# Output projection of a hybrid decoder block: a fifth pair of weight tiles by seven products, its loads and two groups of small attention products moved

## The chip, the cores and the metric

The kernel runs on one core of one Trainium2 chip. The core has a matrix engine (TensorE, PE in the profile; its weight loads are PEld), a vector engine (VectorE, DVE), a scalar engine (ScalarE, ACT), GpSimd (POOL), a synchronizing engine (SyncE, SP) that here issues nearly all loads, and 16 DMA engines. The metric is the device time in microseconds of the whole program, as the median of several runs; lower is better.

## The reference

One decoder block on 256 tokens of width 2048, all in float32. The part that matters here:

```python
proj = x @ w_in                       # split into GLA q/k/v/gate, FoX q/k/v/forget, two merge gates
y_gla = o @ w_branch_gla              # gated linear attention, 4 heads
y_fox = of @ w_branch_fox             # forgetting attention, 8 heads, softmax with a bias from cumsum(log f)
merged = sigmoid(ma) * y_gla + sigmoid(mb) * y_fox
mix = merged @ w_out                  # the output projection, 2048 x 2048
x = layer_norm(ALPHA * x + mix, ln1_g, ln1_b)
ffn = conv_gated_mlp(x, ...)          # w_gate, w_up: 2048 x 5632, w_down: 5632 x 2048
x = layer_norm(ALPHA * x + ffn, ln2_g, ln2_b)
x = x + sigmoid(x @ w_ple_gate) * (p @ w_ple_proj)
```

## The kernel before

**Precision and tiles.** Every large product is made of three products in the type fp32r: each operand is split into a high part (`copy` on ScalarE writes `hi`) and the rest (`tensor_tensor` on VectorE writes `lo`), and hi*hi, hi*lo and lo*hi are summed. The weights stream through SBUF as units of 128 x 2048 values (`wu`, 1 MB). `unit()` (line 235) hands out the next unit and first prepares those up to three ahead (`prep`, line 191): SP loads two raw tiles of 128 x 1024 into a ring of four, ScalarE makes hi, VectorE lo.

**Two kinds of large product.** `w_unit` (lines 290 and 292) has the weights as the stationary operand: for each of 16 blocks one matmul of hi against 512 columns (high and low part of the activations) and one of lo against 256. The input projections (tiles psfq, psfk, psq, psk, psm), the branches (psa, psb) and the feed-forward's gate and up use it. `x_mm` (line 334) has the activations as the stationary operand and weight rows of 512 columns as the moving one; values, output gates, the output projection (wo) and the down projection (dn) use it, through `x_half`, which does 1024 output columns at a time in four PSUM banks, two token blocks by two column blocks. In `x_half` a unit is a pair of 128-row blocks of the weights; a half of the output projection is 8 pairs.

**A pair by seven products.** A pair is a 2 x 2 by 2 x 2 block product, 8 block products of 3 matmuls, 24 in all. For the pairs listed in `WOW` for the output projection and `DNW` for the down projection, `seven` (line 354) computes it by seven block products of 3 matmuls, in Strassen's manner. That needs sums of the activation blocks (`x_sums`, line 363, made in the branch loop when the pair's second block is done, and kept in `msums`, two tiles of two pairs each), combined weights, and four more PSUM tiles `ms`, which gather over the half's listed pairs and are added into the residual z by `joined` (lines 1095 to 1117) after the last of them. The output projection's combined weights are made during the loop over the merge gates: `combs_gen` (line 896) takes three calls per listed pair: load 1 MB (combw, SP), two subtractions, a third one and a store to DRAM (tfd, POOL's queue). It is called once per gate column block from number 17 on, 32 in all, then in the branch loop. `prep_seven` (line 142) then loads, for such a pair, 256 KB (rawl), 512 KB (raw) and the 1 MB of combined weights (full), in that order, and splits them into hi, lo and two tiles ts.

**Buffers.** One tag, S8, has 15 buffers of 128 x 2048 values. During the output projection it holds the merged activations mT (4), one tile of sums ms1, the tiles full and ts of listed pairs (1 and 2 each), the two token blocks z1 of the residual, the normalization's gain and bias rows (lnb, 2), later its output x1T (4). Another, t2, has six buffers of 128 x 512.

**The order of the work.** The instructions of all engines but SP are put in order by a scheduler at build time, by priority (the order of the program) and by when it expects operands and buffers. SP's instructions stay in program order. What is to happen between pairs is given to `x_half` as a table `mid`: the entry of pair i runs after pair i's products were issued. In line 1268 these are, for the output projection's first half, the loads of the residual's two token blocks (`mid1`, SP) after pairs 2 and 3 and of the gain row (`mid1g`, POOL's queue) after pair 6; for the second half the bias row after pair 1 and other loads after pair 3.

**The small products.** While the large projections run, `pull(1)` after each unit advances a list of generators. `gates_gen` (line 599) does one GLA head's decay gates per call (psg, line 579, two small fp32r products each) and, in a call after the four heads, `fox_columns` (line 562): two fp32 transposes (pct) of the cumulative forget gate and a copy on ScalarE. `fox_gen` (line 609) sweeps the eight heads of the forgetting attention: in the call of head h it transposes its weights (`turn`, pt), forms the logits of head h + 1 (pl) and the value products of head h - 1 (`values`, po); two calls per head, so that the last head's value products have a call of their own, two units after its transposes.

Of the kernel before, what the change touches and what calls it, by code (L numbers as in the profile page):

```python
# [10 lines left out]
F32R = mybir.dt.float32r  # L11
# [8 lines left out]
P = 128  # L20
# [4 lines left out]
H = 4  # L25
DK = 256
FH = 8
# [18 lines left out]
DNP = (1, 2, 4, 5, 7, 8, 10, 11, 13, 14, 16, 18)  # L46
DNW = (DNP, DNP[1:-1])
WO0 = 120
WOW = ((1, 2, 4, 5), ())
WOP = tuple(sorted(set(WOW[0] + WOW[1])))  # L50
COMBW = 17
COMB0 = 13
# [12 lines left out]
def tile_block(ctx: ExitStack, tc: tile.TileContext, wu, xw, wfv, wpp, xT_in, x_in, pT_in, wlr,  # L65
# [7 lines left out]
    sm = ctx.enter_context(tc.tile_pool(name="sm", bufs=2))  # L73
# [9 lines left out]
    st1 = [cst.tile([P, 4, 6], F32, name=f"st1{t}") for t in range(2)]  # L83
# [53 lines left out]
    tsd = dr.tile([len(units7), P, 1024], F32, name="tsd")  # L137
    units7w = [WO0 + nh * 8 + i for nh in range(2) for i in WOW[nh]]
    tsw = {u: j for j, u in enumerate(units7w)}
# [422 lines left out]
    def fox_columns():  # L562
        pct = mxtile("pct")
        for t in range(2):
            nc.tensor.transpose(pct[:, 8 * t:8 * t + FH], zc_[:, t * P:t * P + P],
                                ident[:FH, :FH])
        copy(ct, pct[:, 0:2 * FH])
# [7 lines left out]
    def gla_gates(h):  # L575
        psg = mxtile(f"psg{h}")
        for c in range(2):
            n = (2 * h + c) * P
            nc.tensor.matmul(psg[:, c * 256:c * 256 + 256], lhsT=wS[:, n:n + P],
                             rhs=gS, start=True, stop=True)  # L580
        z = t2("z")
        for c in range(2):
            nc.scalar.activation(z.rearrange("p (t c n) -> p t c n", t=2, c=2)[:, :, c, :],
                                 psg[:, c * 256:c * 256 + 256].rearrange("p (t n) -> p t n", t=2),
                                 AF.Identity, scale=1.0,
                                 bias=chn[:, c_blr + 2 * h + c:c_blr + 2 * h + c + 1])
        g = t2("g")
        log_sigmoid(z, g, P, 512)
        nc.vector.tensor_tensor_scan(gb[:, h, 0:256], reset, g[:, 0:256], 0.0,
                                     ALU.mult, ALU.add)  # L590
        b1 = gb[:, h, 256:512].rearrange("p (c n) -> p c n", n=P)
        nc.vector.tensor_tensor_scan(gb[:, h, 257:512], reset[:, 0:255], g[:, 256:511], 0.0,
                                     ALU.mult, ALU.add)
        nc.vector.memset(b1[:, :, 0:1], 0.0)
        nc.vector.tensor_tensor(gt[:, h, :, :], b1[:, :, 127:128],
                                g[:, 256:512].rearrange("p (c n) -> p c n", n=P)[:, :, 127:128],
                                ALU.add)

    def gates_gen():
        for h in range(H):  # L600
            gla_gates(h)
            yield
        fox_columns()

    mixers.append(gates_gen())

# [2 lines left out]
    def fox_gen():  # L609


        lgs, sts, ptss = {}, {}, {}
        halves = ((256, 128), (0, 256))

        def logits(h):
            pl = mxtile(f"pl{h}")
            for t, (o, n) in enumerate(halves):
                nc.tensor.matmul(pl[:, o:o + n], lhsT=fq[:, h, t * P:t * P + P],
                                 rhs=fk[:, h, 0:n], start=True, stop=True)
            lg = lgs[h] = t2("lg")[:, 0:384]  # L620
            for t, (o, n) in enumerate(halves):
                nc.vector.scalar_tensor_tensor(lg[:, o:o + n], pl[:, o:o + n],
                                               ct[:, t * FH + h:t * FH + h + 1],
                                               ncb[:, h * 256:h * 256 + n], ALU.add, ALU.add)
            nc.vector.tensor_tensor(lg[:, P:384], lg[:, P:384], cmask, ALU.add)
            st = sts[h] = sm.tile([P, 8], F32, tag="fst", name="fst")
            nc.vector.tensor_reduce(st[:, 0:1], lg[:, 256:384], AX.X, ALU.max, negate=True)
            nc.vector.tensor_reduce(st[:, 1:2], lg[:, 0:256], AX.X, ALU.max, negate=True)

        def softmax(h):  # L630
            lg, st = lgs[h], sts.pop(h)
            for t, (o, n) in enumerate(halves):
                nc.scalar.activation(lg[:, o:o + n], lg[:, o:o + n], AF.Exp,
                                     bias=st[:, t:t + 1], scale=1.0,
                                     accum_out=st[:, 2 + t:3 + t])
            nc.vector.reciprocal(st[:, 4:6], st[:, 2:4])
            for t, (o, n) in enumerate(halves):
                nc.vector.tensor_scalar(lg[:, o:o + n], lg[:, o:o + n], st[:, 4 + t:5 + t],
                                        None, ALU.mult)

        def turn(h):
            lg = lgs.pop(h)
            pt = mxtile(f"pt{h}")
            for i, d in enumerate((1, 2, 0)):
                nc.tensor.transpose(pt[:, d * P:d * P + P], lg[:, i * P:i * P + P], ident)
            pts = ptss[h] = t2("pts")[:, 0:384]
            copy(pts, pt[:, 0:384])

        def values(h):
            pts = ptss.pop(h)  # L650
            po = mmtile(f"po{h}")
            nc.tensor.matmul(po[:, 0:256], lhsT=fv[:, 0, h * P:h * P + P], rhs=pts[:, 0:256],
                             start=True, stop=False)
            nc.tensor.matmul(po[:, 128:256], lhsT=fv[:, 1, h * P:h * P + P],
                             rhs=pts[:, 256:384], start=False, stop=True)
            dst = ofT[h // 4][:, h % 4, :]
            copy(dst[:, 0:256], po[:, 0:256])
            nc.vector.tensor_tensor(dst[:, 256:512], po[:, 0:256],
                                    dst[:, 0:256].bitcast(F32), ALU.subtract)

        logits(0)
        yield
        softmax(0)
        yield
        for h in range(FH + 1):
            if h < FH:
                turn(h)
            if h + 1 < FH:
                logits(h + 1)
            if h > 0:  # L670
                values(h - 1)
            if h + 1 < FH:
                softmax(h + 1)
            yield
            yield

# [18 lines left out]
    for nm, dst, sc in (("q", gq, 1.0 / 16.0), ("k", gk, 1.0)):  # L695
        for n in range(8):
# [3 lines left out]
            h, c = n // 2, n % 2  # L700
# [224 lines left out]

    msums = [lt([P, 2, 2, 512], F32R, "hT10"), s8([P, 2, 2, 512], F32R, name="ms1")]

    def m_sums(i):
        j = WOP.index(i)
        return msums[j // 2][:, j % 2, 0, :], msums[j // 2][:, j % 2, 1, :]  # L930

    for nh in range(2):
# [3 lines left out]
    mT = [s8([P, 4, 512], F32R, name=f"mT{i}") for i in range(4)]  # L936
    fhl = None
    ya_even = None
    for n in range(16):
# [6 lines left out]
        j = n % 2  # L946
# [197 lines left out]
    def ple_prep(half):  # L1144

        if half == 0:
            praw = s8([P, 2, 1024], name="praw")
        w = [s8([P, 2048], F32R, name=f"pw{half}{i}") for i in range(2)]
        pt_ = s8([P, 2, 512], F32R, name=f"pTs{half}")
        pTs = [pt_[:, k, :] for k in range(2)]  # L1150
        for k in range(2):
            if half == 0:
                raw = praw[:, k, :]
            else:
                raw = ring.tile([P, 1024], F32, tag="raw", bufs=4, name=f"praw{half}{k}")
            nc.sync.dma_start(raw, wpp[half, :, k * 1024:k * 1024 + 1024])
            o = slice(k * 1024, k * 1024 + 1024)
            copy(w[0][:, o], raw)
            nc.vector.tensor_tensor(w[1][:, o], raw, w[0][:, o].bitcast(F32), ALU.subtract)
        pT = t2("pTr").rearrange("p (k t) -> p k t", t=S)  # L1160
        nc.sync.dma_start(pT, pT_in)
        for k in range(2):
            copy(pTs[k][:, 0:256], pT[:, k, :])
            nc.vector.tensor_tensor(pTs[k][:, 256:512], pT[:, k, :],
                                    pTs[k][:, 0:256].bitcast(F32), ALU.subtract)
        return w, pTs

    z1 = [s8([P, 2048], name=f"z1{t}") for t in range(2)]
    gain = [None, None]

    def mid1(t):
        nc.sync.dma_start(z1[t], x_in[t])
# [3 lines left out]
    def mid1g(i):  # L1176
        gain1.append(load_row(0, i))

    x1T = []
    pq, first = [], []  # L1180

    def mid1x():
        x1T.extend(s8([P, 4, 512], F32R, name=f"x1T{g}") for g in range(4))
# [81 lines left out]
                    turn1(G[3])  # L1265
            first.extend(ps)

    residual("wo", mT, 16, z1, st1, ({2: lambda: mid1(0), 3: lambda: mid1(1), 6: lambda: mid1g(0)}, {1: lambda: mid1g(1), 3: lambda: (pq.append(ple_prep(0)), mid1x())}), end=end1, ws=WOW)
    mixers.append(affine(z1, gain[0], lambda t: nc.gpsimd.dma_start(x1d[t], z1[t]),
                         [g for g in range(4) if g not in AFF_DVE]))  # L1270

# [99 lines left out]
    pb, pq = [], []  # L1371
# [224 lines left out]
```

## Time and profile before

| | |
|---|---|
| median of three runs | 1652.53 us (1652.47 to 1653.07) |
| the profiled execution's own time | 1651.61 us |
| its span in the profile | 1649.8 us |
| TensorE busy | 1643.6 us |
| TensorE weight loads / VectorE / ScalarE busy | 1426.9 / 1233.6 / 882.2 us |
| granted TensorE clock | full speed (1.0) |

A profile is one execution. The page gives each engine's busy time, the chain of work that ended last and the costliest groups of instructions. Other views of the same trace, which the prediction uses: the waits of an engine (who waited for whom), the instructions in order of time (start, duration, engine, line, operation, output <- input, count; in brackets the idle time before and what ended it), the busy time in given stretches, and the DMA issues with size and time to landing. A matmul's duration reaches into the next one, since matmuls are pipelined; the distance between two starts is what one costs.

### The profile page before, as it was taken

To read this page: it belongs to the slowest core of one execution; us is meant where nothing else is said; L and a number is where in the kernel's file an instruction comes from. 1 tells how busy PE (TensorE), PEld (TensorE's weight loads), DVE (VectorE), ACT (ScalarE), POOL (GpSimd) and SP (SyncE) were. 2 spreads that over 40 slices of the span, in tenths; PEclk is the share of its full clock that TensorE was granted. 3 is DMA by queue.
4 is the path that set the end of the run, shared out by engine and by line. 5 is a ranking of instruction groups with operands and counts; after the bars stand their busy time and mean duration, and the time that the engine had idled before them with its cause. 6 is when DMAs were issued, how large, how long until landed. Compare 5 with 4: busy or idle time off the path is not lost.

```text
span 1649.8 us, 24319 instructions
## 1 busy us (share of the span) xinstructions
PE 1643.6 (100%) x8956; PEld 1426.9 (86%) x8956; DVE 1233.6 (75%) x1819; ACT 882.2 (53%) x1268; POOL 94.8 (6%) x219
## 2 busy tenths in 40 slices
PE   9999999999999999999999999999999999999998
PEld 8988888888888888888888888888888888888887
DVE  6666658668856667786888778888887688788784
ACT  6745545445555455555565545555455566466643
POOL 0000000000000000000010011111110011010000
PEclk9999999999999999999999999999999999999999
DMA  7765555555555685668747678889886589799354
GB/s 299 233 196 189 168 186 178 183 179 179 174 180 195 242 307 192 193 206 316 267 155 234 232 257 334 316 325 337 322 285 229 192 292 325 270 329 363 141 187 170
DMA packets 107527, 394.23 MB, mean 239 GB/s; under 512 B 12504, under 2 KB 13408, under 8 KB 104464
## 3 DMA queue, kind: packets, MB, share of 16 engines
q1 hardware_dynamic: 97008, 352.62, 62.0%
q0 software_dynamic: 10256, 39.86, 6.3%
q8 instruction: 70, 1.15, 0.3%
q14 instruction: 49, 0.40, 0.1%
q10 hardware_dynamic: 144, 0.20, 0.0%
HBM read 365.36 MB, written 27.27 MB: 238 GB/s over the span
## 4 chain that ended last, share of the span: by engine, by line
PE 96%; DMA 2%; ACT 1%; DVE 1%; issue 0%; SPq 0%; ACTq 0%
PE psu L290 9%; PE psg L290 9%; PE dn L334 7%; PE psm L290 7%; PE gv L334 5%; PE gr L334 5%; PE pg L334 5%; PE psu L292 5%; PE psg L292 5%; PE psm L292 4%; PE psa L290 3%; PE wo L334 3%; PE dn L354 3%; PE fv L496 3%; PE dn0m L354 2%; PE psfq L290 2%
## 5 line engine op out<-in xcount | busy, mean ns | idle before, releaser
L217 DVE TENSOR_TENSOR lo<-raw,hi 128x1024 fp32r<-128x1024 f32 x502 | 611.5, 1224 | 271.9 <-ACT hi L212 270.3
L212 ACT ACTIVATE hi<-raw 128x1024 fp32r<-128x1024 f32 x502 | 528.7, 1059 | 465.4 <-DMA raw<-in_wu_dram 114.6
L290 PE MATMUL psu<-x1T,hi 128*128 128x512 f32 x688 | 236.0, 389 | 0.0
L290 PE MATMUL psg<-x1T,hi 128*128 128x512 f32 x672 | 230.5, 389 | 0.0
L292 PE MATMUL psu<-x1T,lo 128*128 128x256 f32 x688 | 189.9, 276 | 0.0
L292 PE MATMUL psg<-x1T,lo 128*128 128x256 f32 x672 | 185.5, 276 | 0.0
L290 PE MATMUL psm<-xT,hi 128*128 128x512 f32 x512 | 175.5, 390 | 0.0
L290 PEld LDWEIGHTS psu<-x1T,hi 128*128 128x128 f32 x688 | 129.1, 188 | 26.7
L290 PEld LDWEIGHTS psg<-x1T,hi 128*128 128x128 f32 x672 | 126.2, 188 | 26.1
L292 PE MATMUL psm<-xT,lo 128*128 128x256 f32 x512 | 141.4, 276 | 0.0
L292 PEld LDWEIGHTS psu<-x1T,lo 128*128 128x128 f32 x688 | 129.2, 188 | 0.0
L292 PEld LDWEIGHTS psg<-x1T,lo 128*128 128x128 f32 x672 | 126.1, 188 | 0.0
L290 PEld LDWEIGHTS psm<-xT,hi 128*128 128x128 f32 x512 | 96.1, 188 | 19.9
L334 PE MATMUL dn<-hi,hT 128*128 128x512 f32 x352 | 97.8, 389 | 0.0
L292 PEld LDWEIGHTS psm<-xT,lo 128*128 128x128 f32 x512 | 96.2, 188 | 0.2
L290 PE MATMUL psa<-oT,hi 128*128 128x512 f32 x256 | 87.8, 389 | 0.0
L334 PEld LDWEIGHTS dn<-hi,hT 128*128 128x128 f32 x352 | 66.0, 188 | 13.7
L292 PE MATMUL psa<-oT,lo 128*128 128x256 f32 x256 | 70.7, 276 | 0.0
L334 PE MATMUL gr<-hi,xT 128*128 128x512 f32 x256 | 70.6, 392 | 0.0
L334 PE MATMUL gv<-hi,xT 128*128 128x512 f32 x256 | 70.4, 391 | 0.0
L334 PE MATMUL pg<-hi,x2T 128*128 128x512 f32 (+1 forms) x224 | 60.0, 376 | 0.0
L290 PEld LDWEIGHTS psa<-oT,hi 128*128 128x128 f32 x256 | 48.1, 188 | 10.1
(357 smaller groups left out, 3070.4 us busy)
## 6 DMA issues: line engine op xcount, KB each, us to landing
raw<-in_wu_dram SPq DMA_DIRECT2D x528, 512.0 KB, 4.9
comb<-in_wu_dram SPq DMA_DIRECT2D x22, 768.0 KB, 8.9
tsd<-comb POOLq DMA_DIRECT2D x22, 512.0 KB, 7.3
top<-tsd SPq DMA_DIRECT2D x22, 512.0 KB, 5.8
fvraw<-in_wfv_dram SPq DMA_DIRECT2D x15, 524.0 KB, 7.9
rawf<-in_wu_dram SPq DMA_DIRECT2D x14, 512.0 KB, 9.5
top<-in_wu_dram SPq DMA_DIRECT2D x22, 256.0 KB, 6.8
hi<-hsd POOLq DMA_DIRECT2D x22, 256.0 KB, 4.9
```

The lines of the kernel that those rows point to most:

```text
L212: c = nc.scalar.activation(hi, raw, AF.Copy, bias=0.0, scale=1.0)
L217: return nc.vector.tensor_tensor(lo, raw, hi.bitcast(F32), ALU.subtract)
L290: nc.tensor.matmul(ps, lhsT=hi[i // 8 if hoff == 0 else 0][:, w0 % 1024:w0 % 1024 + P], rhs=a[:, kt % 4, :], start=first and i == 0, stop= ...
L292: nc.tensor.matmul(ps[:, 256:512], lhsT=lo[i // 8 if hoff == 0 else 0][:, w0 % 1024:w0 % 1024 + P], rhs=a[:, kt % 4, 0:256], start=False, ...
L334: nc.tensor.matmul(bs[j][:, 0:m], lhsT=x, rhs=v[:, o:o + m], start=first and i == 0, stop=last and i == 2)
L354: nc.tensor.matmul(ps, lhsT=a, rhs=v, start=m and first and i == 0, stop=m and last and i == 2)
L496: nc.tensor.matmul(fbk[t][c][:, 0:n], lhsT=x, rhs=w[:, o:o + n], start=kt == 0 and i == 0, stop=kt == 15 and i == 2)
```

## The change

The list of the output projection's first half gains pair 6. Its activation sums get two tiles of the tag t2 (`ms2`), its weights are combined in a fifth round of `combs_gen`, and its four extra PSUM tiles go on gathering for one more pair, so that `joined` runs after pair 6 and not after pair 5. In the table of the output projection's loads, both token blocks of the residual move to after pair 4, the gain row to after pair 0 of the second half, the bias row to after its pair 2. `fox_columns` runs ahead of the last head's gates, in the same call. The last head's value products are issued in the call of its own transposes, so `fox_gen` ends one head step sooner.

```diff
-WOW = ((1, 2, 4, 5), ())
+WOW = ((1, 2, 4, 5, 6), ())
...
     def gates_gen():
         for h in range(H):
+            if h == H - 1:
+                fox_columns()
             gla_gates(h)
             yield
-        fox_columns()
...
-        for h in range(FH + 1):
-            if h < FH:
-                turn(h)
+        for h in range(FH):
+            turn(h)
             if h + 1 < FH:
                 logits(h + 1)
             if h > 0:
                 values(h - 1)
             if h + 1 < FH:
                 softmax(h + 1)
+            else:
+                values(h)
             yield
             yield
...
+    ms2 = [sm.tile([P, 512], F32R, tag="t2", bufs=6, name=nm) for nm in ("ms2h", "ms2l")]
+
     def m_sums(i):
         j = WOP.index(i)
+        if j == 4:
+            return ms2
         return msums[j // 2][:, j % 2, 0, :], msums[j // 2][:, j % 2, 1, :]
...
-    residual("wo", mT, 16, z1, st1, ({2: lambda: mid1(0), 3: lambda: mid1(1), 6: lambda: mid1g(0)}, {1: lambda: mid1g(1), 3: lambda: (pq.append(ple_prep(0)), mid1x())}), end=end1, ws=WOW)
+    residual("wo", mT, 16, z1, st1, ({4: lambda: (mid1(0), mid1(1))}, {0: lambda: mid1g(0), 2: lambda: mid1g(1), 3: lambda: (pq.append(ple_prep(0)), mid1x())}), end=end1, ws=WOW)
```

## The prediction

> **What bounds the kernel now.** I read the page first, then TensorE's waits, then TensorE's instructions in order of time around the output projection, and last the queues and engines that feed it there.
>
> ```profile
> span 1649.8 us, 24319 instructions
> ...
> PE 1643.6 (100%) x8956; PEld 1426.9 (86%) x8956; DVE 1233.6 (75%) x1819; ACT 882.2 (53%) x1268; POOL 94.8 (6%) x219
> ...
> PE 96%; DMA 2%; ACT 1%; DVE 1%; issue 0%; SPq 0%; ACTq 0%
> ```
>
> ```profile
> PE wo L334 <- DVE lo L217: 0.2, 1, 0.2
> ```
>
> TensorE is busy for all but 6.2 us of the span and holds 96% of the chain that ends last. So two things shorten this kernel: fewer products, or products that follow each other faster. One of TensorE's few waits lies where the change works (wo). A busy TensorE can still hide short delays, so I use the distances between starts.
>
> ```profile
> 754.48 0.39 PE L354 MATMUL wo<-hi,hT 128*128 128x512 f32 x1
> ...
> 759.24 0.39 PE L354 MATMUL wo<-hi,hT 128*128 128x512 f32 x1
> ...
> 764.00 0.62 PE L334 MATMUL wo<-hi,mT 128*128 128x512 f32 x2
> ...
> 769.44 0.39 PE L354 MATMUL wo<-hi,ms 128*128 128x512 f32 x1
> ...
> 778.96 1.07 PE L334 MATMUL wo<-hi,mT 128*128 128x512 f32 x4
> ...
> 782.57 0.73 PE L334 MATMUL wo<-lo,mT 128*128 128x512 f32 x2 [0.21 <-DVE lo L217]
> ...
> 784.52 1.07 PE L334 MATMUL wo<-hi,mT 128*128 128x512 f32 x4
> ```
>
> Pair 1 (seven products) runs from 754.48 to 759.24 and pair 2 to 764.00: 4.76 us each, 21 matmuls of 0.227. Pair 3, plain, runs to 769.44: 5.44 us, 24 matmuls of 0.227. Pair 6, plain, starts at 778.96; its 23rd matmul starts at 784.52, 5.56 later, where 22 x 0.227 = 4.99 are due. So pair 6 loses 0.57 us, more than the 0.2 that the waits show.
>
> **Pair 6 by seven products: TensorE.** It drops from 24 matmuls to 21: 3 x 0.227 = **-0.68 us**, on the path, since nothing but matmuls fills it. The Trainium skill (TensorE: Matmul & The Clock Gate, section Back-to-back issue gap) gives about 131 ns per matmul of 512 columns as a sustained rate in real kernels; by it the term would be an estimated -0.39. The rows above, 4.76 over 21 and 5.44 over 24, do not agree with that figure, and the rows decide.
>
> **Pair 6: the stall of 0.57.** Where does it come from?
>
> ```profile
> 755.97 0.42 SPq L1172 DMA_DIRECT2D z<-in_x_dram  x1
> ...
> 759.97 0.44 SPq L149 DMA_DIRECT2D full<-tfd  x1
> 760.46 0.43 SPq L1172 DMA_DIRECT2D z<-in_x_dram  x1
> 760.99 34.09 SPq L205 DMA_DIRECT2D raw<-in_wu_dram  x12
> ```
>
> ```profile
> 766.38 1.07 POOL L1138 DMA_DIRECT2D lnb<-in_lng_dram  x2 [171.24 <-DVE ts L160]
> ```
>
> ```profile
> 760.00:765.00 5.00, 5.00 (x24) 4.14 (x23) 2.97 (x4) 2.83 (x3) 0.00 (x0) 1.00 1.01 415
> ...
> 775.00:780.00 5.00, 5.00 (x24) 4.02 (x23) 1.23 (x1) 1.06 (x1) 0.00 (x0) 1.00 1.00 413
> ```
>
> ```profile
> 780.20 1.06 ACT L212 ACTIVATE hi<-raw 128x1024 fp32r<-128x1024 f32 x1 [1.70 <-DMA raw<-in_wu_dram]
> ...
> 783.61 0.58 ACT L1109 ACTIVATE ju<-wo0m 128x512 f32<-128x512 f32 x1
> ```
>
> The last two columns of the stretches are the DMA engines' share and their GB/s: they are full, at some 415 GB/s, while pair 6's raw tiles, issued at 760.99, stand behind the two z (the residual's token blocks) and pair 5's full tile, and beside two rows lnb (the normalization's gain and bias); its second half reaches ScalarE only at 780.20. The change moves both z loads (SP) behind pair 6's own loads and ahead of pair 7's, and both lnb loads to the second half. Those are on POOL's queue, whose 171 us of idle time before them show that nothing stands behind them.
>
> ```profile
> raw<-in_wu_dram SPq DMA_DIRECT2D x53, 512.0 KB, 4.9
> full<-tfd SPq DMA_DIRECT2D x4, 1024.0 KB, 7.1
> z<-in_x_dram SPq DMA_DIRECT2D x2, 1024.0 KB, 11.0
> ...
> rawl<-in_wu_dram SPq DMA_DIRECT2D x4, 256.0 KB, 5.6
> ```
>
> Pair 6 now brings raw 0.5 + rawl 0.25 + full 1.0 = 1.75 MB instead of 1.0, but has lost 2 MB of z in front: 1.25 MB less, at 415 GB/s 3.0 us earlier than the 780.2 above.
>
> ```profile
> L217 DVE TENSOR_TENSOR lo<-raw,hi 128x1024 fp32r<-128x1024 f32 x502 | 611.5, 1224 | 271.9 <-ACT hi L212 270.3
> ```
>
> So its last tile lands by 777.2 even if lnb goes out as early as now, and up to 2/0.415 = 4.8 us before that if not. Its four splits of 1024 columns take 1.06 each on ScalarE and 1.22 on VectorE, side by side; the last two (ts), ready by 777.2 + 1.06 + 2 x 1.22 = 780.7, are first read by the tenth matmul, at 778.96 + 9 x 0.227 = 781.0. **The stall goes: -0.57.** Next to be late is pair 7, with 0.75 MB more ahead of it, 1.8 us if lnb goes as early as now. Its raw tiles follow those at 780.2, its need is 778.96 + 4.76 = 783.72: up to 0.5 us could come back. I take 0.
>
> **Joining moves one pair later.** The first of its operations is ScalarE's copy ju (L1109). It ran at 783.61, 4.65 after pair 5's end at 778.96, since it stood behind the late raw tiles in ScalarE's order. Pair 6 now ends at 783.72, so it can start where it started.
>
> ```profile
> 787.82 0.68 DVE L1106 TENSOR_TENSOR ju<-ju,wo0m 128x512 f32<-128x512 f32 x1
> ```
>
> The second PSUM bank that the next half needs comes free with the read at 787.82, at 788.5. The next half began at 790.41 (784.97 + 5.44) and would begin at 789.16: 0.66 us of cover instead of 1.9. I take 0, and 0.5 for the range.
>
> **What pair 6 adds off the path.** Another combine pass (1 MB in, 1 MB out, three VectorE operations) on the last three rounds of the gate loop; its sums on VectorE and ScalarE in the branch loop, whose tiles ms2 take two of six t2 buffers that nothing else needs there.
>
> ```profile
> 600.00:610.00 10.00, 10.00 (x61) 8.86 (x60) 6.42 (x8) 5.41 (x8) 0.00 (x0) 1.00 0.81 296
> 736.00:745.00 9.00, 9.00 (x55) 7.98 (x54) 7.12 (x12) 5.96 (x9) 0.00 (x0) 1.00 0.80 274
> ```
>
> ```profile
> L363 DVE TENSOR_TENSOR msf<-ya x8: 291/292/293, 646.7 to 720.1; 128x128 f32<-128x128 f32 x8
> ...
> L969 DVE SCALAR_TENSOR_TENSOR ms<-msf,ms x2: 684/684/684, 707.8 to 724.1; 128x512 fp32r<-128x512 f32 x2
> ```
>
> The sums are 4 x 0.29 + 0.68 = 1.85 us on VectorE, which stands idle 1.9 of the 9 us from 736 to 745: hidden, barely. The pass has 19% of the DMA engines free from 600 to 610. Both at 0; without cover 0.5 each.
>
> **The order of the small products.** The two fp32 transposes of the forget columns (pct) move one round up, beside the last gates; the last head's value products (po) move up beside its transposes. No product is added or dropped. But the trace shows what a visit of such products can leave behind:
>
> ```profile
> L290 PE MATMUL psfq<-xT,hi 128*128 128x512 f32 x46 | 16.1, 395 | 0.0
> L292 PE MATMUL psfq<-xT,lo 128*128 128x256 f32 x46 | 12.9, 280 | 0.0
> ```
>
> ```profile
> L290 PE MATMUL psk<-xT,hi 128*128 128x512 f32 x31 | 10.9, 395 | 0.0
> L292 PE MATMUL psk<-xT,lo 128*128 128x256 f32 x31 | 8.7, 280 | 0.0
> ```
>
> ```profile
> L290 PE MATMUL psk<-xT,hi 128*128 128x512 f32 x75 | 25.5, 389 | 0.0
> L292 PE MATMUL psk<-xT,lo 128*128 128x256 f32 x74 | 20.4, 276 | 0.0
> ```
>
> These are the same matmuls from 82 to 104 (behind pct), from 204 to 214.6 (behind the visit of turn and values) and from 217 to 242 (behind the last visit). In the first two windows a pair of hi and lo takes 6 + 4 = 10 ns longer, and it stays so until another visit. The 46 + 31 = 77 pairs cost 0.77 us; psfq is followed by psfk in the first window, so I count about 1 us in all. What sets it I can't read from the trace; it follows the visits, and the change alters just these two.
>
> ```profile
> 80.62 0.28 PE L565 MATMUL pct<-ident,zc 8*128 8x8 f32 x2
> 80.84 0.50 PE L290 MATMUL psfq<-xT,hi 128*128 128x512 f32 x1
> ```
>
> The visit itself costs 0.22 us and a first matmul 0.11 longer than 0.39; sharing a visit saves 0.1 to 0.2 at each place, unless the values wait for ScalarE's copy of the transposes and become a visit of their own again. Bounds: best -1.3 (both slow stretches gone, visits shared); worst, the last visit leaves the slow pace on the 75 pairs that now run fast: +0.75, say 0.8. I take **-0.5**, half of the slow pace gone.
>
> **The sum**, against the profiled execution's own 1651.61 (span 1649.8 and 1.81 around it): -0.68 - 0.57 - 0.5 = -1.75, so 1649.9. The runs' median, 1652.53, lies 0.92 above that execution; the same step down gives **1650.8**.
>
> **The rivals.** *The slow pace stays or spreads* (for: nothing in the trace says which order is quick; against: the last visit, values alone, leaves the fast pace): -1.25 with 0 to +0.8, up to 1652.1. *The stall only moves to pair 7 or to the banks* (for: covers of 0.7 us; against: lnb's 2 MB leave the stretch): -0.68 and the small products, 1651.4 to 1652.3. *Slower: a z load waits for its buffer.* z, full and ts share one tag of 15 buffers, SP issues in program order, and the two lnb rows waited for just such a buffer (row at 766.38). If z waits for pair 5's ts, free when pair 6 starts (778.96), then pair 7's raw follows at 779.4, lands 4.9 later and is split 1.06 and 1.22 later: lo at 786.6, where pair 7's third matmul wants it at 784.2: 2.4 us. z lands at 778.96 + 11.0 = 790, so joining starts 6.2 us late, the bank is free at 794.7, and the next half, due at 789.16 + 2.4 = 791.6, loses 3.1 more. That is -0.68 - 0.57 + 5.5 = +4.25: 1656.8. It hurts once z goes out after about 774. Against it: 15 less mT's 4 and ms1's 1 leaves 10, and at 760 only about 7 are held. *A cold clock on top of that:*
>
> ```profile
> L128 PE MATMUL warm_ps<-warm x8: 380/631/631, 1.2 to 4.1; 128*128 128x512 bf16 x8
> ```
>
> The kernel's first eight matmuls of 512 columns start 2.9/7 = 0.41 us apart instead of 0.227, so a stall long enough to bring that back costs about 7 x 0.19 = 1.3 us more: +5.55, 1658.1. The Trainium skill (the same page, section Part 1: The HAM clock gate) has the clock fall to half after an idle window of about 3.4 us; no stretch of this trace shows it behind a stall. *The change doesn't do it:* pair 6 stays plain, 0; the code excludes it but for a slip.
>
> **Chances.** Forecast 0.61, slow pace 0.20, moved stall 0.11, buffer wait 0.05, cold clock 0.02, no change 0.01. Over 0.2%, 3.3 us, which is about what a measurement of this kernel can tell from no change, lie only the buffer wait and the cold clock, 0.07; the best sum of bounds, -0.68 - 0.57 - 1.3 = -2.55, doesn't reach it on the other side, so faster gets 0.03 for what I don't see; same 0.90. The range: low end at that best sum, 1650.0, less 0.2 for the runs' own spread; high end past the second and third case, 1653.0, which leaves out some 0.1.
>
> **What would show it.** Right: line 354's matmuls in the output projection go from 4 x 21 = 84 to 105; pair 6's start to pair 7's is 4.76; the wait on lo at wo is gone; psfq and psk show 389 and 276 throughout. Wrong: a TensorE wait on z's chain (z, ju) or on raw at pair 7, lnb or z issued after 774, groups at 395 and 280 that last longer than before, or a lead lost in the branch loop's first units.

## The result, and the profile after

The changed kernel is slower: 1656.30 us median (9 runs, 1653.74 to 1657.46) against 1652.34 us for the kernel before on the same chip (9 runs, 1651.65 to 1653.07). The ratio is 1.0024, with a 95% interval of 1.0013 to 1.0034. The forecast was 1650.8 with a high end of 1653.0. The profiled execution took 1656.13 us.

The page of the changed kernel, its span, its engines' busy times and the chain that ended last:

```profile
span 1654.4 us, 24332 instructions
...
PE 1644.8 (99%) x8953; PEld 1427.8 (86%) x8953; DVE 1238.2 (75%) x1829; ACT 884.5 (53%) x1271; POOL 94.9 (6%) x220
...
PE 93%; DMA 3%; DVE 2%; ACT 1%; issue 1%; SPq 0%; POOL 0%; ACTq 0%; DVEq 0%
```

Three TensorE instructions fewer are there, as forecast; yet the span is 4.6 us longer, and TensorE's share of the chain fell from 96% to 93%. TensorE's waits in the changed kernel from 50 us on (total, times, longest):

```profile
PE wo L334 <- ACT hi L212: 1.6, 1, 1.6
PE ptl L1062 <- DVE lny L1074: 0.9, 1, 0.9
PE po L653 <- ACT pts L116: 0.8, 1, 0.8
PE wo L334 <- DVE lo L217: 0.5, 1, 0.5
...
```

The kernel before had one wait of 0.2 at wo; the line left out, 0.2 at ptl, both kernels have. Four new ones stand here, in three places. I measure each place by the distance between the first matmuls of two stages: from psfq to gv the small attention products run; from wo to ptl the output projection; from ptl to psu the first normalization (ptl holds its transposes, psu belongs to the feed-forward behind it).

| distance of starts, us | before | after | difference |
|---|---|---|---|
| psfq to gv | 190.48 | 192.53 | +2.05 |
| wo to ptl | 84.94 | 86.58 | +1.64 |
| ptl to psu | 10.11 | 11.21 | +1.10 |

With -0.2 in the rest that is the 4.6.

**The output projection.** TensorE's instructions in order of time, changed kernel:

```profile
781.03 0.39 PE L354 MATMUL wo<-hi,ms2h 128*128 128x512 f32 x1
...
785.11 0.84 PE L354 MATMUL wo<-ts,mT 128*128 128x512 f32 x3
787.58 0.73 PE L334 MATMUL wo<-hi,mT 128*128 128x512 f32 x2 [1.63 <-ACT hi L212]
788.84 0.73 PE L334 MATMUL wo<-lo,mT 128*128 128x512 f32 x2 [0.53 <-DVE lo L217]
```

Pair 6 starts at 781.03 and its last three matmuls at 785.11, so it would end at 785.79: 4.76 us, without a stall. Pair 7 starts at 787.58, 1.79 late, its third matmul loses another 0.70, and the first matmul after each wait is 0.11 longer: 2.7 us. The instructions of all engines around it show why:

```profile
764.90 1.69 SPq L1178 DMA_DIRECT2D z<-in_x_dram  x2
...
767.89 21.25 SPq L205 DMA_DIRECT2D raw<-in_wu_dram  x5
...
773.18 0.55 POOL L1144 DMA_DIRECT2D lnb<-in_lng_dram  x1 [162.06 <-DVE ts L160]
775.37 0.54 POOL L1144 DMA_DIRECT2D lnb<-in_lng_dram  x1 [1.65 <-PE wo0m L354]
786.47 1.06 ACT L212 ACTIVATE hi<-raw 128x1024 fp32r<-128x1024 f32 x1 [8.87 <-DMA raw<-in_wu_dram]
```

Pair 7's raw tiles were issued from 767.89 on and reached ScalarE at 786.47, after it had been idle for 8.87 us. The two lnb rows went out at 773.18 and 775.37: not after pairs 0 and 2 of the second half, where the table has them, but as soon as a buffer came free (the brackets name its last users, ts and wo0m). The DMA queues of the changed kernel from 777 to 784.5 (packets, MB, share of the 16 engines), q0 POOL's and q1 SP's:

```profile
q0 software_dynamic: 260, 1.98, 62.5%
q1 hardware_dynamic: 262, 1.18, 37.8%
```

And of the kernel before from 770 to 777.5, when its pair 6 waited:

```profile
q0 software_dynamic: 266, 2.03, 64.4%
q1 hardware_dynamic: 283, 1.11, 35.9%
```

Both queues send nearly the same number of packets, but lnb's lines have 8 KB (2048 values) and raw's 4 KB, so POOL's queue gets almost two thirds of the bytes, and nearly all of lnb's 2 MB goes through ahead of the raw tiles. Before, pair 6's tiles came late that way (e9 below); now pair 7's. The Trainium skill (DMA: Bandwidth & Descriptors, section Queues, rings and completion order) says that each DMA engine serves the queues in turn, a packet at a time. These counts, 260 against 262, agree with it, if the trace's packets, here mostly a line each, stand for the page's.

**The normalization.** VectorE in order of time, first before, then changed:

```profile
825.32 1.23 DVE L217 TENSOR_TENSOR lo<-raw,hi 128x1024 fp32r<-128x1024 f32 x1 [1.37 <-ACT hi L212]
826.46 0.68 DVE L1092 SCALAR_TENSOR_TENSOR z<-z,wo 128x512 f32<-128x512 f32 x1
```

```profile
831.07 1.23 DVE L217 TENSOR_TENSOR lo<-raw,hi 128x1024 fp32r<-128x1024 f32 x1 [2.52 <-ACT hi L212]
832.21 0.68 DVE L1098 SCALAR_TENSOR_TENSOR z<-z,wo 128x512 f32<-128x512 f32 x1
```

The last lo split stands ahead of the residual (z) and its statistics. It ran 8.64 us before the first transposes (833.96) in the kernel before, 6.59 before them (837.66) in the changed one, and the chain behind it gets to lny, the read of ptl that the third group of transposes waits for, 0.9 us too late.

**The small products.** TensorE in order of time in the changed kernel, at the last head's visit:

```profile
203.22 0.60 PE L653 MATMUL po<-pts,fv 128*128 128x256 f32 x2
203.65 0.38 PE L655 MATMUL po<-pts,fv 128*128 128x128 f32 x2
204.79 0.70 PE L653 MATMUL po<-pts,fv 128*128 128x256 f32 x2 [0.75 <-ACT pts L116]
```

The values now wait 0.75 for ScalarE's copy of the transposes made just ahead of them. The rest of this stage's +2.05 is mostly pace: behind this visit the matmuls of psk run at 395/280 ns to the end of psk, where the kernel before ran at 389/276 from 217 on (rows below).

### The profile page after: what moved, and what is told of

It is laid out like the page before. It is cut to its first block, busy times and chain, and to the rows that moved or that the text cites. A ratio compares the mean times of both kernels' runs of the same rounds, so it can differ in the third digit from the quotient of the medians.

```text
span 1654.4 us, 24332 instructions
## 1 busy us (share of the span) xinstructions
PE 1644.8 (99%) x8953; PEld 1427.8 (86%) x8953; DVE 1238.2 (75%) x1829; ACT 884.5 (53%) x1271; POOL 94.9 (6%) x220
## 4 chain that ended last, share of the span: by engine, by line
PE 93%; DMA 3%; DVE 2%; ACT 1%; issue 1%; SPq 0%; POOL 0%; ACTq 0%; DVEq 0%
PE psu L290 9%; PE psg L290 9%; PE dn L334 7%; PE psm L290 7%; PE gv L334 5%; PE gr L334 5%; PE pg L334 5%; PE psu L292 5%; PE psg L292 5%; PE psm L292 4%; PE psa L290 3%; PE dn L354 3%; PE fv L496 3%; DMA raw<-in_wu_dram 2%; PE dn0m L354 2%; PE psk L290 2%
```

## The experiments

Each kernel was run beside the kernel before on the same chip. Each median is of 11 runs but e11's. "Difference" is from the median of the kernel before, run beside it. Run e12 is the kernel before itself, and its difference shows how far such a median can be off. Where the interval holds 1, as for e1, e3, e4, e8, e9 and e12 (e2's ends there), the time is not clearly another than before; the distances, of one profiled execution each, then say more than the median.

| run | median, us | difference | ratio, 95% interval | psfq to gv | wo to ptl | ptl to psu |
|---|---|---|---|---|---|---|
| e1_order | 1652.68 | +0.43 | 0.9991 to 1.0008 | 191.44 | 84.35 | 10.11 |
| e2_pair6 | 1653.85 | +1.60 | 1.0000 to 1.0018 | 190.48 | 86.36 | 10.11 |
| e3_lnb_sp | 1652.69 | +0.44 | 0.9993 to 1.0010 | 191.45 | 83.67 | 10.70 |
| e4_pair6_lnb_sp | 1653.22 | +0.97 | 0.9995 to 1.0013 | 191.00 | 84.49 | 11.81 |
| e5_after | 1654.83 | +2.78 | 1.0007 to 1.0025 | 190.66 | 86.07 | 11.06 |
| e6_lnb_4k | 1654.52 | +2.47 | 1.0007 to 1.0025 | 190.52 | 86.30 | 10.10 |
| e7_values_apart | 1654.06 | +2.01 | 1.0002 to 1.0020 | 190.74 | 85.98 | 10.96 |
| e8_lnb_early | 1651.61 | -0.44 | 0.9990 to 1.0007 | 191.00 | 83.67 | 10.14 |
| e9_before_lnb_sp | 1651.72 | -0.94 | 0.9990 to 1.0008 | 190.78 | 84.35 | 10.11 |
| e10_both | 1650.68 | -1.98 | 0.9979 to 0.9997 | 190.73 | 83.68 | 10.10 |
| e11_z_behind (5 runs) | 1657.52 | +4.86 | 1.0019 to 1.0044 | 190.53 | 91.08 | 10.11 |
| e12_before | 1652.06 | -0.60 | 0.9988 to 1.0006 | 190.99 | 85.03 | 10.20 |

**The two halves of the change.** e1_order is the kernel before with the new order of the small products alone; e2_pair6 is the changed kernel with the old order.

> The kernel before with the new order of the small products alone (forget columns ahead of the last gates, the last head's values in the call of its own transposes); four pairs by seven products as before. Theory 1: the order alone costs what the changed profile shows up to the first product of gv, about +2.1 us: a TensorE wait of about 0.8 us in po on ScalarE's copy of the transposes, and groups of psfk, psq and psk at 395 and 280 ns after every second visit. So about +2.1 us (+0.13%) against before. Rival: the pace after a visit is a matter of chance in each execution and not of the order; then the wait of 0.8 stays, the pace differs from execution to execution, and the mean is +0.5 to +1.5 us.

> The changed kernel with the old order of the small products: pair 6 by seven products and the moved loads alone. Theory 1: what is left is the output projection's part, a stall of about 2.7 us at pair 7 and about 1.1 us more at the first normalization, less 0.68 and 0.57: about +2.5 us against before, and 2.1 us less than the changed kernel. Rival (the order is harmless, the loss is all at the output projection): +4 us, like the changed kernel.

The order alone gave +0.43, not +2.1: its first theory falls. The 0.7 wait on pts was there. Pair 6 alone gave +1.60 and the waits at wo:

```profile
PE wo L334 <- ACT hi L212: 1.0, 1, 1.0
PE wo L334 <- DVE lo L217: 0.5, 1, 0.5
```

So most of the loss seems to come with pair 6 and its loads, and in this execution none of it in psfq to gv. The two halves make +2.0 together, less than the change's own +4.0 and, in e5, +2.8; their intervals allow for that. e1 also showed that the stall of pair 6 comes and goes: with before's loads, wo to ptl was 84.35 there, 0.59 less than in before's profile.

**lnb off POOL's queue.** e3_lnb_sp is the changed kernel, e4_pair6_lnb_sp the one with the old order, each with lnb issued by SP at the same places of the table, so behind what SP issues there:

```diff
-        q = nc.gpsimd if li == 0 else nc.sync
+        q = nc.sync
```

> The changed kernel with the gain and bias rows of the first normalization issued from SP's queue, at the same places of the program, instead of POOL's queue; nothing else. Theory 2: in the changed profile these 2 MB go out at 773 and 775, long before the place they are written at, and take 240 to 295 of 420 GB/s from 777 to 784 while pair 7's raw tiles are due; on SP they go out in program order, after 788. Then the stall at pair 7 (2.7 us) and most of the extra wait at the normalization (1.1 us) go: 3 to 3.8 us less than the changed kernel, so between -0.5 and +1 us against before. Rival: the two z loads ahead of pair 7 are enough to make it late; then a stall of 1 to 2.5 us at pair 7 stays, and the gain over the changed kernel is under 1.5 us.

> Both at once: pair 6 by seven products and the moved loads, the old order of the small products, and the gain and bias rows from SP's queue. Theories 1 and 2 together: no stall at pair 7, so -0.68 and -0.57 remain: about -1.2 us against before (-0.07%). Rivals: if z alone makes pair 7 late, about +0.5 to +1.5; if the order is harmless, the same as the kernel with the rows on SP and the new order.

In both, every wait at wo is gone, and in e3 wo to ptl is 83.67, 2.9 less than after: with z ahead of it as in the change, lnb on POOL's queue is what made pair 7 late. But e4 gained nothing in the median, against my expectation. Its waits:

```profile
PE ptl L1060 <- DVE lny L1072: 1.8, 1, 1.8
PE ptl L1060 <- ACT z L1052: 0.7, 1, 0.7
```

SP issued lnb at 786 and 801, ahead of the raw tiles of the last pairs, and ptl to psu grew by 1.7. e3 issued it at the same two moments and paid 0.6 there, so the size of this loss differs between executions.

**Is it the packets?** e5_after is the changed kernel again. e6_lnb_4k loads each lnb row in two halves, still on POOL's queue:

```diff
-        q.dma_start(row, lng[2 * li + i].broadcast_to([P, 2048]))
+        for o in range(0, 2048, 1024):
+            q.dma_start(row[:, o:o + 1024], lng[2 * li + i, :, o:o + 1024].broadcast_to([P, 1024]))
```

> The changed kernel once more, profiled anew beside the others. Theory 2 (lnb's 2 MB share the DMA engines with pair 7's raw tiles): the waits at wo on hi L212 and lo L217 come back, 1.6 + 0.5 us, and the stretch from wo's start to ptl is 1.0 to 1.7 us longer than before's 84.94; median +3 to +4 us. Rival (the first profile showed a chance stall, as before's pair 6 had one that was absent in another run): no such wait here, median +1 to +2 us. The pace from psfq to gv: if the order sets it, +2.05 us again; if chance sets it, some other figure between +0.9 and +2.1.

> The changed kernel with each lnb row loaded in two pieces of 1024 columns, still on POOL's queue: the same bytes at the same places in lines of 4 KB, as raw has them, instead of 8 KB. Theory 3 (the DMA engines take the two queues' packets in turn, so that the queue with the larger packets gets two thirds of the bytes): POOL's queue falls from some 260 to about 210 GB/s while both have work, SP's rises from 150 to about 210, pair 7's raw tiles land about 2 us sooner, and TensorE's wait at wo falls from 2.1 us to 0.5 or less; median 1.5 to 2.5 us less than the changed kernel on this chip. Rival (the share goes by queue, or by who issued first, not by packet): the split and the wait stay, median within 0.5 us of the changed kernel.

e5 had the waits at wo again (0.9 on hi, of which 0.3 in the second half, and 0.5 on lo), though psfq to gv was 1.9 shorter than in the first profile. In e6 the queues from 777 to 784.5 were:

```profile
q1 hardware_dynamic: 426, 1.59, 51.7%
q0 software_dynamic: 427, 1.55, 50.6%
```

Again equal packets, and now nearly equal bytes. Only the length of lnb's lines differs, and with it the number of its loads, four for two; so a share by queue, or for whoever issued first, is ruled out: the queues take turns by packet here, and the longer line gets more. Pair 7's first raw tile came to ScalarE at 782.29, and both waits on hi and lo are gone. But the time is not; its waits show one in their place:

```profile
PE wo L334 <- DVE z L1117: 2.1, 1, 2.1
```

L1117 is the read in the joining that frees a PSUM bank for the second half. ScalarE's instructions in e6 show what held it:

```profile
782.29 1.06 ACT L212 ACTIVATE hi<-raw 128x1024 fp32r<-128x1024 f32 x1 [6.90 <-DMA raw<-in_wu_dram]
784.76 1.06 ACT L212 ACTIVATE hi<-raw 128x1024 fp32r<-128x1024 f32 x1 [1.41 <-DMA raw<-in_wu_dram]
787.02 1.06 ACT L212 ACTIVATE hi<-raw 128x1024 fp32r<-128x1024 f32 x1 [1.20 <-DMA raw<-in_wu_dram]
788.43 1.06 ACT L212 ACTIVATE hi<-raw 128x1024 fp32r<-128x1024 f32 x1 [0.35 <-PE wo L334]
789.39 0.58 ACT L1115 ACTIVATE ju<-wo0m 128x512 f32<-128x512 f32 x1
```

The joining's first copy, ju, could have run when pair 6 ended, at 784.2. It stands in ScalarE's order behind the last three of these splits of raw tiles, two of which wait for DMA. VectorE's order adds a little: L1117 reads no ju, and yet runs at 791.26, behind a lo split and the first addition to ju. The median fell by only 0.3 against e5: the mechanism was as expected, the gain was not.

**The values alone.** e7_values_apart is the changed kernel with the last head's values in their own call, so that only pct stays moved.

> The changed kernel with the last head's value products back in a call of their own; only the forget columns (pct) stay moved. Theory 1 (the values wait for ScalarE's copy pts, 0.7 to 0.8 us, and cost what they were to save): the wait po on pts is gone and the stretch from psfq to gv is 0.9 to 1.1 us shorter than the changed kernel's on this chip, so about 0 to +1 against before; median about 1 us less than the changed kernel. Rival (the moved pct sets the slow pace): the wait is gone, and the stretch keeps +0.9 or more by pace alone.

The wait on pts is gone, and the median is 0.8 below e5's, but the intervals overlap. psfq to gv did not get shorter than e5's, because the pace differed: the visits before this one left groups at 395/280 in e7 and at 389/276 in e5.

**lnb early on SP's queue.** e8_lnb_early has pair 6, the old order, lnb on SP, and this table (against the changed kernel's):

```diff
-... ({4: lambda: (mid1(0), mid1(1))}, {0: lambda: mid1g(0), 2: lambda: mid1g(1), 3: ...
+... ({4: lambda: (mid1(0), mid1(1)), 6: lambda: mid1g(0), 7: lambda: mid1g(1)}, {3: ...
```

> Pair 6 by seven with the small products in the old order, and the two lnb rows on SP's queue, in program order after pairs 6 and 7 of the first half: behind pair 7's raw tiles and ahead of the second half's, where the tiles have a lead. Theory 2: no wait at wo, pair 6 gains 0.68 and the old stall of pair 6 is gone; with lnb out of the way before the last pairs, the raw tiles of the normalization's stretch come in time and the 1.7 us that the late lnb cost there (ptl waiting for lny) goes too: median 1650.8 to 1651.5, 0.8 to 1.5 less than before. Rival (the normalization waits because VectorE's last lo splits stand ahead of the statistics, whatever lnb does): ptl still waits 1 us or more, and the median is within 0.5 us of before or above it.

SP issued lnb at 774.21 and 784.89, behind pair 7's raw tiles. No wait at wo, and ptl waits 0.2 us in all: against e4, where only these places differ, wo to psu is 2.5 shorter, and against e3, 0.6. The median, 1651.61, is just above the expected 1650.8 to 1651.5, and its step of -0.44 falls short of the expected 0.8 to 1.5 and is not clear of noise.

**What is left for pair 6, and the parts that pay.** e9_before_lnb_sp is the kernel before with lnb on SP after pairs 6 and 7; e10_both is e8 with fox_columns moved as in the change.

> The kernel before, only with the two lnb rows on SP's queue, in program order after pairs 6 and 7 of the first half, as in the run that had pair 6 by seven and the old order. Theory 4 (lnb on POOL's queue is what made pair 6 late in before; all that pair 6 by seven itself brings is 0.68): no wait at wo here, the stretch from wo's start to ptl 84.4 us, median 0 to 0.6 us below before, and that run's 1.1 to 1.3 us shorter stretch leaves 0.6 to 0.7 for pair 6. Rival (z and full ahead of pair 6's raw tiles are enough to make it late): the wait of 0.2 us or more on lo at wo stays.

> Pair 6 by seven, lnb on SP's queue after pairs 6 and 7, the forget columns moved beside the last gates, the last head's values in their own call: the parts of the change that pay, without those that cost. Theory: the stretch from psfq to psfk is 45.07 to 45.2 (it was 45.07 to 45.08 in four of the five runs with the columns moved, 45.55 or 45.1 in those without), no wait at wo or ptl over 0.3 us; median 0.8 to 1.7 us below before. Rival (the pace of the attention's stretch is drawn anew in each execution and takes the rest): the stretch at wo is as short, but the median lies within 0.5 us of before.

e9's stage is 84.35, e8's and e10's 83.67 and 83.68: pair 6 by seven is worth 0.67 to 0.68 once nothing stalls. That e9 has no wait at wo would prove little, since e1 had none either. Its raw tiles say more; this is the second half of pair 6's, in e9:

```profile
774.53 1.06 ACT L212 ACTIVATE hi<-raw 128x1024 fp32r<-128x1024 f32 x1 [1.41 <-DMA raw<-in_wu_dram]
```

That is 4.55 ahead of the pair's first matmul (779.08). With lnb on POOL's queue and the same other loads it came 1.24 (before), 0.64 (e1) and 0.94 (e12) behind that matmul: late each time, and a few tenths of a us decide whether TensorE waits. e9's median, -0.94, goes beyond the expected 0 to 0.6, but is not clear of noise.

From e10's TensorE rows, the last matmuls of pair 6 and the first of pair 7:

```profile
783.60 0.84 PE L354 MATMUL wo<-ts,mT 128*128 128x512 f32 x3
784.28 0.62 PE L334 MATMUL wo<-hi,mT 128*128 128x512 f32 x2
784.73 0.62 PE L334 MATMUL wo<-lo,mT 128*128 128x512 f32 x2
```

Nothing lies between them. e10 is the only run whose interval lies below 1: 1650.68, ratio 0.9988 (0.9979 to 0.9997). What it has over e8, the moved columns, is not shown to pay: psfq to psfk takes 45.07 in e10 and 45.12 in e8, and the two medians were not taken side by side.

**z behind pair 7, and before once more.** e11_z_behind is the changed kernel with both z loads after pair 5 in place of pair 4.

> The changed kernel with both z loads one pair later, behind pair 7's raw tiles, lnb still on POOL's queue. If only lnb's share made pair 7 late, and z's 2 MB ahead of it did not matter, pair 7's raw tiles are still late and TensorE waits 1 us or more on hi L212 at wo. If the two add up (my theory): pair 7's raw tiles land some 5 us sooner and that wait is gone, but z's 2 MB now share with lnb and land after 784, so that the joining starts late and TensorE waits 1 to 4 us at wo on z (L1117) for its PSUM bank; median within 1.5 us of the changed kernel's, not better than before.

> The kernel before once more, with a profile of its own. If the pace of the small-product stretch and the stall of pair 6 belong to the order of the instructions, psfq to gv is 190.48 again and the wait on lo at wo 0.2 us. If they are drawn anew in each execution (my theory since the changed kernel gave 192.53 and 190.66), at least one of them differs: psfq to gv by 0.3 us or more, or the wait is absent. The median is the same as before's, 1651.5 to 1652.7.

In e11 pair 7 came in time, with lnb still on POOL's queue. So lnb and z add up: pair 7 is late with both ahead of it, and in time with lnb gone from there (e3) or z behind it (e11). The wait at the bank was worse than in any other run:

```profile
PE wo L334 <- DVE z L1117: 2.5, 1, 2.5
PE wo L334 <- DVE ju L1112: 1.8, 1, 1.8
```

The median is +4.9 from before, 0.9 and 2.1 above the changed kernel's two steps (+4.0 and +2.8), where I had expected at most 1.5. I had also expected late z loads to hold the joining. Issued from 768.36 on, they took 12.5 and 16.9 us, so the later one was there at about 786. But ju, the joining's first step, reads no z; as in e6 it stood in ScalarE's order behind raw tiles, which came late with z's 2 MB now ahead of them, after 9.48 us of idle time, and ran at 789.56:

```profile
787.39 2.26 ACT L212 ACTIVATE hi<-raw 128x1024 fp32r<-128x1024 f32 x2 [9.48 <-DMA raw<-in_wu_dram]
789.56 0.58 ACT L1115 ACTIVATE ju<-wo0m 128x512 f32<-128x512 f32 x1
```

The waits explain 4.7 us (the distances 2.91 and 2.24 where 0.227 are due), but the stage is 7.4 longer than e10's. Its stretches (the last three columns are the granted TensorE clock, the DMA share and GB/s):

```profile
790.00:792.50 2.50, 0.24 (x1) 0.19 (x1) 2.50 (x4) 2.11 (x3) 0.00 (x0) 1.00 0.53 170
792.50:795.00 2.50, 0.73 (x2) 0.50 (x2) 2.50 (x4) 1.06 (x1) 0.00 (x0) 0.64 0.70 265
795.00:797.50 2.50, 2.50 (x7) 1.92 (x6) 2.50 (x5) 1.06 (x1) 0.00 (x0) 0.50 0.77 226
797.50:800.00 2.50, 2.50 (x7) 1.92 (x7) 2.50 (x5) 0.00 (x0) 0.00 (x0) 0.50 0.57 185
800.00:805.00 5.00, 5.00 (x23) 4.12 (x23) 5.00 (x8) 1.24 (x2) 0.00 (x0) 1.00 0.11 30
```

After the wait the clock is at half: eleven matmuls are 0.43 apart instead of 0.227, 2.2 us more, and the one ahead of them and the one behind lose 0.5. e12, the kernel before again, has no wait on lo of 0.2, but short stalls at 782.94, in pair 6, and at 795.46, in the second half, instead (0.25 and 0.37), and a different pace, psfq to gv 190.99.

## Why the prediction was wrong, point by point

- **Pair 6, -0.68:** right. Line 354 has 105 matmuls in wo (84 before), the pair takes 4.76, and the stages without a stall differ by 0.67 to 0.68.
- **The stall of pair 6, -0.57:** it went, but it was no fixed cost: absent in e1, and in e12 0.25, with 0.37 more in the second half. The term took what one execution showed for a cost of the kernel.
- **"Next to be late is pair 7 ... up to 0.5 us could come back. I take 0":** this step failed. It came to 2.7 us in the first profile and 1.7 in e5, where the second half lost another 0.6 to late tiles. Two premises were wrong. "lnb's 2 MB leave the stretch" read the table as the time of issue; on POOL's queue the rows went out when a buffer came free, at 773 and 775, later than before's 766.38 and still ahead of pair 7's raw tiles, as the share by packets then let nearly all of lnb pass first. And the bound of 0.5 was too small even for that case. Its bytes were about right: pair 7's first raw tile reached ScalarE 32.39 after wo's start in the kernel before (781.41), and 34.36 after it in e5 (783.87), 2.0 later where 0.75 MB at 415 GB/s make 1.8; in the first profile it was 3.0 later, 35.39. But the bound stops at the start of the pair. The third matmul wants lo, which VectorE makes in 1.22 behind hi, and that came to another 0.7 in both executions; the prediction counted this step for a late z and left it out here. e3 takes lnb away and the waits go; e6 evens the lines out and the waits on hi and lo go; e11 puts z behind pair 7 and they go too.
- **Joining, 0, cover 0.66:** no wait in the changed kernel's two profiles, since pair 7 was late itself. e6 and e11 show the cover to be too small as soon as pair 7 is in time but the next pair's raw tiles are late: 2.1 and 4.3 us, by way of ScalarE's order. The prediction named that order, for ju in the kernel before, and did not carry it over.
- **The small products, -0.5:** failed. The exception that the text named ("unless the values wait for ScalarE's copy of the transposes") is what happened, 0.7 to 0.8 us in every run with the values merged. And the slow pace could not be forecast from one execution. Of the two slow windows that the prediction names, the first did become fast (psfq to psfk 45.07 against 45.55), but so it was in e12 without any change (45.11). From psfq to gv the changed kernel gave 192.53 and 190.66, the kernel before 190.48 and 190.99. The groups of psk from 217 to 243 in the changed kernel's two executions, first profile and e5:

```profile
L290 PE MATMUL psk<-xT,hi 128*128 128x512 f32 x76 | 26.6, 395 | 0.0
L292 PE MATMUL psk<-xT,lo 128*128 128x256 f32 x75 | 21.0, 280 | 0.0
```

```profile
L290 PE MATMUL psk<-xT,hi 128*128 128x512 f32 x78 | 26.6, 389 | 0.0
L292 PE MATMUL psk<-xT,lo 128*128 128x256 f32 x77 | 21.3, 276 | 0.0
```

- **The normalization:** in no term of the sum, and worth +1.1. With the change's loads it came in the first profile, e5 and e7 (11.21, 11.06, 10.96), and not in e2 (10.11), so it is no fixed cost either. With lnb on SP's queue, ptl to psu is 10.70 and 11.81 where it goes out late (e3, e4), 10.14 and 10.10 where it goes out early (e8, e10). That the late raw tiles do it in the changed kernel is read from its trace and not tried by itself.
- **The rivals:** the moved stall was the right one, priced at 1651.4 to 1652.3 instead of 1656.3. z did not wait for a buffer (764.90, row above). The cold clock came in no run but e11. The time that the prediction gave for a wait at the bank with a cold clock was 1658.1; e11 measured 1657.52, with the waits and the half clock in its trace, but in another kernel and by another chain: what held the joining was ScalarE's order and not a late z. That the two times lie close is chance.

What sets the two paces stays open. The first comparison's +4.0 and e5's +2.8 differ by 1.2, about as much as the spans of their profiled executions, 1654.4 and 1653.1.

## What to carry to other kernels

Look up when a load really goes out: here, on a queue that nothing else filled, it left when its buffer came free, whatever its place in the table, and so landed on the next tile in need. When a wait for a tile is priced, follow it to the last consumer of its split parts, not to the first. When two queues are busy, price the needed one by its share, and see whose lines are longer. Before a term is taken at zero, follow the in-order engine that would serve the next consumer: in e6 splits that wait for DMA held up a copy whose input was ready five microseconds earlier.

## What the runs showed of the hardware

Two DMA queues that both had work sent nearly equal numbers of packets: 260 and 262 with lines of 8 and 4 KB (1.98 and 1.18 MB), 427 and 426 with lines of 4 KB (1.55 and 1.59 MB).

In e11 the granted clock fell to 0.50 although no single wait of TensorE was longer than 2.5 us: two waits, 2.5 and 1.8, with one matmul between them. The Trainium skill (TensorE: Matmul & The Clock Gate, section Part 1: The HAM clock gate) has the clock fall after an idle window of about 3.4 us; here the two waits together were longer than that, though a matmul lay between them, and in e6 a single one of 2.1 left the clock at 1.00. Over what stretch the clock's gate counts, no run here shows.

The same instructions in the same order ran at 395/280 ns per pair of hi and lo in one execution and at 389/276 in another, for the 26 us from 217 to 243 (first profile and e5).
